# Low parts of three weights by accumulating transfers, and a new order of steps, in the first tiles of a ConvFFN

## The chip, the cores and the metric

The kernel runs on one core of one Trainium2 chip. The metric is the device time of one execution in microseconds (us); lower is better. Beside each other on the core work TensorE (matrix products; PE in the profile), VectorE (DVE), ScalarE (ACT), GpSimd (POOL) and SyncE (SP). The last issues most of the transfers between the chip's large memory and its working memory; GpSimd issues some.

## The reference

One step of a decoder layer in float32: an adaptive norm, one wide projection that feeds a short gated convolution and a windowed attention, a gated merge, a residual, and then the part that matters here, the ConvFFN, followed by a last norm:

```python
h2 = _rmsnorm(x, norm2_g) * (1.0 + sc2) + sh2
a, val = jnp.split(h2 @ w_up, 2, axis=-1)
ac, new_ffn = _causal_conv(a, ffn_buf, ffn_conv_w)
x = x + g2 * ((jax.nn.gelu(ac, approximate=False) * val) @ w_down)
```

There are 512 prompt tokens and 64 sample tokens (8 sequences of 8), 576 columns together. The model width is 1024, the inner width 2816, so `w_up` has 2 x 2816 columns: 22 gate tiles `a` and 22 value tiles `val` of 128 columns each. The causal convolution has three taps.

## The kernel before

**Products of split numbers.** TensorE multiplies numbers of a shortened float32 form (`F32R`). To keep the accuracy of float32, each operand is split into a high part (its rounding to that form) and a low part (the number minus the high part), and each product is made of three passes: high by high, high by low, low by high (`kstep`, with the weight's low part in the third pass). For a weight tile of 128 x 1024 the high part is one ScalarE pass (`whi` in the profile) and the low part one VectorE subtraction (`wlo`).

**Tiles.** Activations lie transposed: 128 features on the partitions, 576 tokens along the row. Weights arrive in tiles `raw` of 1024 x 128 (512 KB), issued by SyncE (`load_w`) into a ring of four buffers, so that a load waits until the last reader of its buffer is done. High and low parts have rings of five. A product of one weight tile with all eight feature tiles of `h2` fills one of two wide accumulators (`mm`); there are four narrow ones (`aux`).

**The stage.** The ConvFFN goes through the 22 tiles in three groups. The tiles 0 to 3 (class `FfnTile`) are plain products. All later ones (`FfnPair`) use a scheme with seven smaller products for a gate tile and a value tile together (`pair_product`, parts 1 to 7), whose operands are sums and differences of halves: of the activations (`PairOperands`, four of them, with `sums`, `high`, `low` and `n3`) and of two weight tiles (`pair_weights`, whose steps `sums1`, `sums2`, `ah`, `al`, `bh`, `bl`, `ch`, `cl`, `dh`, `dl` make the high (h) and low (l) parts of four weight sets A to D). Beside the products of the tiles 0 to 3, VectorE and ScalarE thus have to finish those tiles, prepare the four operands, and prepare the weights of pair 4.

A plain tile needs, in turn: `copies` (ScalarE takes the gate product from its accumulator into a padded row; GpSimd clears and fills the padding and keeps the convolution's state), `first_tap` (ScalarE), `taps` (two VectorE instructions), `gelu` (ScalarE), `times` (VectorE multiplies by the value product out of its accumulator), `high` (ScalarE) and `low` (VectorE). The helpers `start` and `value` are `copies` with `first_tap`, and `times` with `high`.

**What comes before.** The gate and value products of tile 0 (`acc2[0]`, `acc2[1]`) and the gate product of tile 1 (`first[2]`) are made while `h2` is still being normalised. Then follow five products over all of `h2`: `v1` (value of tile 1), `a2`, `v2`, `a3`, `v3` (gate and value of tiles 2 and 3), and after them pair 4. The weights of `v1` and `a2` are split early; those of `v2`, `a3` and `v3` in the stage itself, by `w_split`. With two wide accumulators, `v1` takes the one that tile 0's `copies` has read, `a2` the one that tile 0's `times` has read, `v2` the one of `v1`, and so on.

**What sets the order.** In this stage the lists of TensorE, VectorE and ScalarE are pinned to the order in which the program is written (`pinned`). Each engine works its list in turn, and an instruction that waits holds up all behind it. GpSimd's order is set by a scheduler at build time.

Of the kernel before, what the change touches and what calls it, by code (L numbers as in the profile page):

```python
# [10 lines left out]
F32 = mybir.dt.float32  # L11
F32R = mybir.dt.float32r
AF = mybir.ActivationFunctionType
ALU = mybir.AluOpType
AX = mybir.AxisListType

P = 128
D = 1024
NK = D // P
# [16 lines left out]
S_BUFS = 5  # L36
# [33 lines left out]
def step_kernel(ctx: ExitStack, tc: tile.TileContext, ins: dict, outs: list):  # L70
# [6 lines left out]
    wp = ctx.enter_context(tc.tile_pool(name="wp", bufs=3))  # L77
# [8 lines left out]
    def nm(s):  # L86
        cnt[0] += 1
        return f"{s}{cnt[0]}"

    def slot(s, dt=F32, shape=None):  # L90
        return ap_.tile(shape or [P, NT], dt, tag="a", name=nm(s))

    def mmps():
        return pm.tile([P, 1024], F32, tag="mm", name=nm("mm"))
# [19 lines left out]
    pe, act, dve, pool = (InOrder(e) for e in (nc.tensor, nc.scalar, nc.vector, nc.gpsimd))  # L114
# [5 lines left out]
    def pf(ps):  # L120
        return ps[:, 256:832]
# [4 lines left out]
    def sv(t):  # L126
        return t[:, 512:576]

    def b8(t):
        return t.rearrange("p (b t) -> p b t", b=8)  # L130
# [4 lines left out]
    def split(hi, lo, src):  # L135

        act.activation(hi, src, AF.Copy)
        dve.tensor_tensor(out=lo, in0=src, in1=hi.bitcast(F32), op=ALU.subtract)
# [6 lines left out]
    def load_w(src, nk):  # L145

        raw = wp.tile([P, nk, P], F32, tag="raw", name=nm("raw"), bufs=W_BUFS)
        nc.sync.dma_start(raw, src)
        return raw

    def split_w(raw):
        nk = raw.shape[1]
        hi = wp.tile([P, nk, P], F32R, tag="whi", name=nm("whi"), bufs=S_BUFS)
        lo = wp.tile([P, nk, P], F32R, tag="wlo", name=nm("wlo"), bufs=S_BUFS)
        split(hi, lo, raw)
        return (lambda k: hi[:, k, :]), (lambda k: lo[:, k, :])

    def split_w_slots(raw):

        nk = raw.shape[1]  # L160
        parts = []
        for k0 in range(0, nk, 4):
            n = min(4, nk - k0)
            hi, lo = slot("wh", F32R, [P, n, P]), slot("wl", F32R, [P, n, P])
            split(hi, lo, raw[:, k0 : k0 + n, :])
            parts.append((hi, lo))
        return (lambda k: parts[k // 4][0][:, k % 4, :]), (lambda k: parts[k // 4][1][:, k % 4, :])
# [11 lines left out]
    def tick():  # L179

        ticks[0] += 1
        if filler:
            filler[2] += filler[1]
            while filler and filler[2] >= 1.0:
                filler[2] -= 1.0
                if next(filler[0], True):
                    filler.clear()
# [6 lines left out]
    def kstep(dst, w, xs, k, groups=(0, 1)):  # L194

        hi, lo = w
        xh, xl = xs[k]
        first, last = k == 0, k == len(xs) - 1
        for wt, x, st, sp_ in ((hi(k), xh, first, False), (hi(k), xl, False, False), (lo(k), xh, False, last)):
            for g in groups:  # L200
                matmul(dst[g], wt, x[:, GRP[g][0] : GRP[g][1]], start=st, stop=sp_)

    def halves(ps):
        return ps[:, 256:512], ps[:, 512:832]

    def product(w, xs):
        ps = mmps()
        for k in range(len(xs)):
            kstep(halves(ps), w, xs, k)
            tick()  # L210
        return pf(ps)
# [17 lines left out]
    class PairOperands:  # L229
# [38 lines left out]
        def low(self):  # L268
            for lo, src, hi in ((self.tl, self.t, self.th), (self.nl, self.r[0][:, :HT], self.nh)):
                dve.tensor_tensor(out=lo, in0=src, in1=hi.bitcast(F32), op=ALU.subtract)  # L270
# [58 lines left out]
    def in_turn(t):  # L329

        order = {0: "sums1 ah al", 2: "dh dl sums2", 3: "bh bl", 4: "ch cl"}
        return {at: (lambda names=names: [t[n]() for n in names.split()]) for at, names in order.items()}
# [46 lines left out]
    def kpm(w, m0, k0=0, nk=NK):  # L379
        return w[k0 * P : (k0 + nk) * P, m0 : m0 + P].rearrange("(k p) m -> p k m", p=P)  # L380
# [7 lines left out]
    first = sp.tile([P, 1], F32, tag="first", name="first", bufs=1)  # L388
# [226 lines left out]
    def early_high(w, x):  # L615
        c, m = slice(4 * x, 4 * x + 4), slice(w * P, w * P + P)
        src = early_q[:, c, :] if w == 2 else early[x][:, :, m]
        hi, lo = wk_parts[w]
        hi, lo = hi[:, c, :], lo[:, c, :]
        act.activation(hi, src, AF.Copy)  # L620
        return lambda: dve.tensor_tensor(out=lo, in0=src, in1=hi.bitcast(F32), op=ALU.subtract)
# [29 lines left out]
    low = early_high(1, 0)  # L651
# [42 lines left out]
    for j in (2, 0, 1):  # L694
        t = slot("kT")
# [20 lines left out]
    for raw in raws:  # L716
        hi = wp.tile([P, 4, 256], F32R, tag="whi", name=nm("whi"), bufs=S_BUFS)
        lo = wp.tile([P, 4, 256], F32R, tag="wlo", name=nm("wlo"), bufs=S_BUFS)
# [14 lines left out]
    for i in range(5):  # L733
        ps = aux()
        for k in range(NK):
            whi, wlo = (x[:, k % 4, :] for x in wv[k // 4])
# [9 lines left out]
    for i in (3, 4):  # L746
# [3 lines left out]
        t = slot("kout", shape=[P, 256])  # L750
# [21 lines left out]
    def queries(t, ps=None):  # L772
# [52 lines left out]
        out=sel,  # L825
        in0=snk.rearrange("p (h g) -> p h g", h=4),
        in1=ind.unsqueeze(1).to_broadcast([P, 4, 4]),
        op=ALU.mult,
# [239 lines left out]
    def b10(t):  # L1068
        return t[:, 514:594].rearrange("p (b e) -> p b e", b=8)
# [105 lines left out]
    for m in range(NK):  # L1175
# [17 lines left out]
        if m == 1:  # L1193
# [9 lines left out]
            out=b10(u)[:, :, 2:10], in0=b8(sv(ps)), in1=b8(sv(c_sb)), op=ALU.mult  # L1203
# [52 lines left out]
    w, steps = pair_weights(*raws[0])  # L1256
    steps = in_turn(steps)
# [12 lines left out]
    def gated(m):  # L1270

        if sg[m] is not None:
            dve.tensor_tensor(out=ya[m], in0=ya[m], in1=sg[m], op=ALU.mult)
            sg[m] = None

    for n in range(len(gate_cols)):
        if n + 1 < len(gate_cols):
            gate_raws(n + 2)
            after, steps = pair_weights(*raws[n + 1])
            steps = in_turn(steps)  # L1280
# [3 lines left out]
        else:  # L1284
            w_next[0] = weights(kpm(wao, 0), NK)
            raw = load_w(kpm(wao, P), NK)
            steps = {
                0: lambda: gated(6), 1: lambda: gated(7), 3: lambda: part_o(2), 4: lambda: part_o(3),
                5: lambda: w_next.update({1: split_w(raw)}), 6: lambda: part_o(5), 7: lambda: part_o(7),
            }  # L1290
# [8 lines left out]
    for m in range(NK):  # L1299
# [5 lines left out]
        t = gb[m]  # L1305
# [62 lines left out]
    h2 = [(slot("2h", F32R), slot("2l", F32R)) for _ in range(NK)]  # L1368
# [216 lines left out]
    def down_load(m, m0, m1):  # L1585
        return load_w(kpm(w_dn, m * P, m0, m1 - m0), m1 - m0)
# [3 lines left out]
    acc2 = [mmps() for _ in range(2)]  # L1590
    first = [halves(x) for x in acc2] + [None]
# [27 lines left out]
    tiles = [FfnTile(m) for m in range(4)]  # L1619
    ops = [PairOperands(h2, kp, made2, h2_raw) for kp in range(4)]  # L1620

    def w_split(raw):
        hi, lo = (wp.tile([P, NK, P], F32R, tag=t, name=nm(t), bufs=S_BUFS) for t in ("whi", "wlo"))
        act.activation(hi, raw, AF.Copy)
        low = lambda: dve.tensor_tensor(out=lo, in0=raw, in1=hi.bitcast(F32), op=ALU.subtract)
        return ((lambda k: hi[:, k, :]), (lambda k: lo[:, k, :])), low

    def start(t, ps):
        t.copies(ps)
        t.first_tap()  # L1630

    def value(t, ps):
        t.times(ps)
        t.high()

    raw = [load_w(kpm(w_up, c), NK) for c in (FF + 2 * P, 3 * P)]
    start(tiles[0], pf(acc2[0]))
    ops[0].sums()
    tiles[0].taps()
    w_v2, low = w_split(raw[0])  # L1640
    tiles[0].gelu()
    low()
    v1 = product(w_v1, h2)
    value(tiles[0], pf(acc2[1]))
    start(tiles[1], first[2])
    tiles[0].low()
    tiles[1].taps()
    for g, k in pend[-1 - NORM2[2] :]:
        norm2_whole(g, k)
    ops[0].high()  # L1650
    tiles[1].gelu()
    w_a3, low = w_split(raw[1])
    raw = load_w(kpm(w_up, FF + 3 * P), NK)
    pair = FfnPair(4)
    ops[0].low()
    ops[1].sums()
    value(tiles[1], v1)
    low()
    ops[1].high()
    a2 = product(w_a2, h2)  # L1660
    tiles[1].low()
    ops[1].low()
    ops[2].sums()
    v2 = product(w_v2, h2)
    start(tiles[2], a2)
    ops[2].high()
    tiles[2].taps()
    w_v3, low = w_split(raw)
    tiles[2].gelu()
    low()  # L1670
    ops[2].low()
    steps = pair.prepare()
    nxt = FfnPair(5)
    ops[3].sums()
    ops[3].high()
    steps["ah"]()
    a3 = product(w_a3, h2)
    value(tiles[2], v2)
    tiles[2].low()
    ops[3].low()  # L1680
    steps["sums1"]()
    steps["al"]()
    steps["dh"]()
    steps["bh"]()
    steps["dl"]()
    v3 = product(w_v3, h2)
    start(tiles[3], a3)
    steps["sums2"]()
    tiles[3].taps()
    tiles[3].gelu()  # L1690
    steps["ch"]()
    steps["bl"]()
    steps["cl"]()
    value(tiles[3], v3)
    tiles[3].low()

# [2 lines left out]
    for m0, m1 in FCH:  # L1699
# [3 lines left out]
        for m in range(max(m0, 4), m1):  # L1703
# [6 lines left out]
            else:  # L1710
                wd = {}
                raw = [down_load(j, m0, m1) for j in range(2)]
# [11 lines left out]
        if m1 < NF:  # L1724
            pairs = {m1: FfnPair(m1)}
            steps = None
# [9 lines left out]
            for m in range(2, NK):  # L1736
# [3 lines left out]
                if m == 4:  # L1740
                    steps = in_turn(pairs[m1].prepare())
# [113 lines left out]
```

## Time and profile before

| | |
|---|---|
| median of 3 runs | 1000.4 us (1000.04 to 1001.07) |
| the profiled execution | 1001.41 us, of it span 999.6 us |
| granted TensorE clock | 0.997 |
| transferred | 119.18 MB, mean 119 GB/s |

The span is the time from the first to the last instruction of one profiled execution; the page of the profile and all queries of the trace belong to that execution. A row of a timeline gives the start, the duration, the engine, the source line, the operation, and the tile written and the tiles read (`out<-in`), with their shape; `x4` merges several like it, and square brackets give the idle time ahead of it and what ended it. Source line 109 is that of a helper through which all pinned engines are called, so tiles tell the instructions apart: `whi` and `wlo` weight parts, `y` the convolution, `cy` the multiplied tile, `fh` and `fl` its parts, `tw`, `th`, `tl` the pair operands, `pad` the padded row, `p` and `uv` the sums inside a pair.

### The profile page before, as it was taken

How to read it: one execution, taken by the hardware profiler on the slowest of the kernel's cores; microseconds unless marked ns; L12 is line 12 of the kernel's file. 1: busy time of each engine (PE TensorE's matmuls, PEld its weight loads, DVE VectorE, ACT ScalarE, POOL GpSimd, SP SyncE). 2: the span in 40 equal slices, each digit the busy share in tenths (PEclk: the TensorE clock that was granted, in tenths of full speed). 3: DMA queues.
4: the chain of work that ended last, by engine and by line, in shares of the span. 5: the costliest groups of instructions: out<-in, count | busy, mean ns of one | idle time of the engine just before them, and what ended most of it. 6: DMA issues, size and time to landing. Idle time of an engine off the chain costs nothing.

```text
span 999.6 us, 18691 instructions
## 1 busy us (share of the span) xinstructions
PE 983.2 (98%) x7516; PEld 941.8 (94%) x7516; DVE 670.7 (67%) x1241; ACT 450.8 (45%) x835; POOL 100.3 (10%) x271
## 2 busy tenths in 40 slices
PE   7999999999999999999999999999999999999997
PEld 5899999999999989999889999999999999999997
DVE  5736676676463348788454568896569995579953
ACT  5454555545334225545232347554225552235453
POOL 2221101020000000000000021011001110001120
PEclk9999999999999999999999999999999999999999
DMA  9984332233421752235972302223233222323302
GB/s 290 319 253 109 86 90 70 86 116 115 141 76 53 246 180 85 86 106 157 338 231 72 106 11 75 65 85 106 85 101 90 85 85 86 106 65 101 110 10 95
DMA packets 173481, 119.18 MB, mean 119 GB/s; under 512 B 6887, under 2 KB 160846, under 8 KB 173106
## 3 DMA queue, kind: packets, MB, share of 16 engines
q1 hardware_dynamic: 169954, 107.00, 35.3%
q0 software_dynamic: 3296, 10.73, 3.5%
q8 instruction: 59, 0.97, 0.4%
q14 instruction: 28, 0.23, 0.1%
q10 hardware_dynamic: 144, 0.26, 0.1%
HBM read 109.17 MB, written 7.35 MB: 117 GB/s over the span
## 4 chain that ended last, share of the span: by engine, by line
PE 82%; DVE 10%; issue 2%; DMA 2%; ACT 2%; SPq 0%; POOL 0%; POOLq 0%; DVEq 0%; ACTq 0%
PE mm L109 60%; PE aux L109 19%; DVE wlo L109 3%; PE aux L1116 2%; DMA ad<-in_w_ada 2%; PE aux L1016 2%; DVE raw L109 1%; DVE uv L109 1%; DVE y L109 1%; DVE cy L109 1%; DMA raw<-in_w_in 1%; DVE fl L109 1%; SPq L385 0%; DVE wl L109 0%; ACT whi L109 0%
## 5 line engine op out<-in xcount | busy, mean ns | idle before, releaser
L109 ACT ACTIVATE whi<-raw 128x1024 fp32r<-128x1024 f32 (+2 forms) x164 | 168.1, 1034 | 178.6 <-PE mm L109 95.5
L109 DVE TENSOR_TENSOR wlo<-raw,whi 128x1024 fp32r<-128x1024 f32 (+2 forms) x164 | 195.1, 1194 | 48.6 <-ACT whi L109 47.9
L109 PE MATMUL mm<-hh,whi 128*128 128x256 f32 (+2 forms) x560 | 124.6, 299 | 0.6 <-ACT hh L109 0.6
L109 PE MATMUL mm<-hh,wlo 128*128 128x256 f32 (+2 forms) x560 | 121.8, 294 | 0.0
L109 PE MATMUL mm<-hl,whi 128*128 128x256 f32 (+2 forms) x560 | 121.0, 295 | 0.1
L109 PEld LDWEIGHTS mm<-hh,whi 128*128 128x128 f32 x560 | 93.0, 188 | 2.9 <-ACT hh L109 1.2
L109 PEld LDWEIGHTS mm<-hh,wlo 128*128 128x128 f32 x560 | 94.2, 188 | 0.0
L109 PEld LDWEIGHTS mm<-hl,whi 128*128 128x128 f32 x560 | 93.6, 188 | 0.5 <-DVE hl L109 0.5
L109 DVE SCALAR_TENSOR_TENSOR x<-mm,modT,x 128x512 f32<-128x512 f32 (+1 forms) x33 | 22.6, 686 | 71.1 <-PE mm L109 71.0
L109 PE MATMUL mm<-fh,whi 128*128 128x256 f32 (+1 forms) x304 | 65.0, 296 | 0.3 <-DVE rt L109 0.3
L109 PE MATMUL mm<-fl,whi 128*128 128x256 f32 (+1 forms) x304 | 65.1, 295 | 0.0
L109 PE MATMUL mm<-fh,wlo 128*128 128x256 f32 (+1 forms) x304 | 64.9, 295 | 0.0
L109 PE MATMUL mm<-th,whi 128*128 128x288 f32 x208 | 61.7, 297 | 0.7 <-DVE uv L109 0.7
L109 PE MATMUL mm<-th,wlo 128*128 128x288 f32 x208 | 61.6, 296 | 0.6 <-DVE wlo L109 0.6
L109 PE MATMUL mm<-tl,whi 128*128 128x288 f32 x208 | 61.4, 295 | 0.0
L109 PEld LDWEIGHTS mm<-fh,whi 128*128 128x128 f32 x304 | 50.7, 188 | 0.5 <-PE mm L109 0.5
L109 PEld LDWEIGHTS mm<-fl,whi 128*128 128x128 f32 x304 | 51.0, 188 | 0.0
L109 PEld LDWEIGHTS mm<-fh,wlo 128*128 128x128 f32 x304 | 50.8, 188 | 0.0
L867 ACT ACTIVATE s<-s,nmx 128x256 f32<-128x256 f32 (+1 forms) x72 | 34.0, 474 | 32.0 <-DVE nmx L864 31.2
L109 PE MATMUL aux<-2h,whi 128*128 128x288 f32 (+2 forms) x160 | 47.2, 295 | 0.8 <-ACT p L109 0.8
L109 PE MATMUL aux<-2h,wlo 128*128 128x288 f32 (+2 forms) x160 | 47.3, 296 | 0.0
L109 PE MATMUL aux<-2l,whi 128*128 128x288 f32 (+2 forms) x160 | 47.0, 294 | 0.0
(310 smaller groups left out, 2568.8 us busy)
## 6 DMA issues: line engine op xcount, KB each, us to landing
raw<-in_w_in SPq DMA_DIRECT2D x52, 512.0 KB, 4.2
raw<-in_w_up SPq DMA_DIRECT2D x44, 512.0 KB, 3.9
ada<-in_w_ada SPq DMA_DIRECT2D x64, 256.0 KB, 6.0
ad<-in_w_ada SPq DMA_DIRECT2D x32, 256.0 KB, 6.3
raw<-in_w_down SPq DMA_DIRECT2D x16, 512.0 KB, 3.5
raw<-in_w_conv_out SPq DMA_DIRECT2D x8, 512.0 KB, 3.5
raw<-in_w_attn_out SPq DMA_DIRECT2D x8, 512.0 KB, 4.2
raw<-in_w_mix_out SPq DMA_DIRECT2D x8, 512.0 KB, 6.1
```

Source lines behind the costliest of these rows:

```text
L109: done = getattr(self.engine, name)(*args, **kwargs)
L867: nc.scalar.activation(s[x // 2][:, x % 2, :w], s[x // 2][:, x % 2, :w], AF.Exp, bias=nmx[:, x : x + 1], accum_out=den[:, x : x + 1],)
L1016: done = nc.tensor.matmul(O[HALF[par], :256], vt(i - nkt + 1 + kt)[:, hd * 64 : hd * 64 + 64], pts[kt][:, par * 256 : par * 256 + 256], st ...
L1116: done = nc.tensor.matmul(ps[32 * j : 32 * j + 32, :], cT[:, k, :], cols[k][j], start=(k == 1), stop=(k == NK - 2),)
```

## The change

The low part of three weights, those of `v2`, `a3` and `v3`, is made another way. ScalarE writes minus the high part into the tile `lo`: a pass over `raw` with scale -1, rounded to the same form. Then GpSimd issues a transfer from `raw` to `lo` that adds what it carries to what lies there. Sum and difference are the same number as before. The third pass of a product now waits for the transfer, and so does the load that takes the buffer of `raw`.

The order of the steps is rewritten from the start of the stage to the pair products. Tile 0 and tile 1 go through their steps side by side; the pair operands and the steps of pair 4's weights are placed anew between the tiles' steps. The order of the products, and with it TensorE's list, remains, as does SyncE's list of loads. GpSimd's list has the padding of tile 1 earlier, and the three transfers: two between the state copies of tile 1 and the padding of tile 2, one between the state copies of tile 2 and the padding of tile 3.

```diff
+    def w_split_adding(raw):
+
+
+        hi, lo = (wp.tile([P, NK, P], F32R, tag=t, name=nm(t), bufs=S_BUFS) for t in ("whi", "wlo"))
+        act.activation(hi, raw, AF.Copy)
+
+        def low():
+            act.activation(lo, raw, AF.Copy, scale=-1.0)
+            pool.dma_start(lo, raw, accum_op=ALU.add)
+
+        return ((lambda k: hi[:, k, :]), (lambda k: lo[:, k, :])), low
...
-    def w_split(raw):
-        hi, lo = (wp.tile([P, NK, P], F32R, tag=t, name=nm(t), bufs=S_BUFS) for t in ("whi", "wlo"))
-        act.activation(hi, raw, AF.Copy)
-        low = lambda: dve.tensor_tensor(out=lo, in0=raw, in1=hi.bitcast(F32), op=ALU.subtract)
-        return ((lambda k: hi[:, k, :]), (lambda k: lo[:, k, :])), low
...
     raw = [load_w(kpm(w_up, c), NK) for c in (FF + 2 * P, 3 * P)]
-    start(tiles[0], pf(acc2[0]))
+    tiles[0].copies(pf(acc2[0]))
+    tiles[1].copies(first[2])
     ops[0].sums()
-    tiles[0].taps()
-    w_v2, low = w_split(raw[0])
-    tiles[0].gelu()
+    for t in tiles[:2]:
+        t.first_tap()
+    for t in tiles[:2]:
+        t.taps()
+    w_v2, low = w_split_adding(raw[0])
+    for t in tiles[:2]:
+        t.gelu()
     low()
     v1 = product(w_v1, h2)
     value(tiles[0], pf(acc2[1]))
-    start(tiles[1], first[2])
-    tiles[0].low()
-    tiles[1].taps()
+    value(tiles[1], v1)
+    ops[1].sums()
+    for t in tiles[:2]:
+        t.low()
+    ops[0].high()
     for g, k in pend[-1 - NORM2[2] :]:
         norm2_whole(g, k)
-    ops[0].high()
-    tiles[1].gelu()
-    w_a3, low = w_split(raw[1])
+    w_a3, low = w_split_adding(raw[1])
+    low()
     raw = load_w(kpm(w_up, FF + 3 * P), NK)
     pair = FfnPair(4)
     ops[0].low()
-    ops[1].sums()
-    value(tiles[1], v1)
-    low()
     ops[1].high()
+    ops[2].sums()
     a2 = product(w_a2, h2)
-    tiles[1].low()
     ops[1].low()
-    ops[2].sums()
-    v2 = product(w_v2, h2)
     start(tiles[2], a2)
     ops[2].high()
     tiles[2].taps()
-    w_v3, low = w_split(raw)
     tiles[2].gelu()
+    w_v3, low = w_split_adding(raw)
     low()
-    ops[2].low()
+    ops[3].sums()
     steps = pair.prepare()
     nxt = FfnPair(5)
-    ops[3].sums()
+    ops[2].low()
+    steps["ah"]()
     ops[3].high()
-    steps["ah"]()
-    a3 = product(w_a3, h2)
+    v2 = product(w_v2, h2)
+    steps["sums1"]()
+    steps["dh"]()
     value(tiles[2], v2)
+    steps["al"]()
+    ops[3].low()
     tiles[2].low()
-    ops[3].low()
-    steps["sums1"]()
-    steps["al"]()
-    steps["dh"]()
     steps["bh"]()
     steps["dl"]()
+    steps["sums2"]()
+    steps["bl"]()
+    a3 = product(w_a3, h2)
+    start(tiles[3], a3)
+    steps["ch"]()
+    tiles[3].taps()
+    steps["cl"]()
+    tiles[3].gelu()
     v3 = product(w_v3, h2)
-    start(tiles[3], a3)
-    steps["sums2"]()
-    tiles[3].taps()
-    tiles[3].gelu()
-    steps["ch"]()
-    steps["bl"]()
-    steps["cl"]()
     value(tiles[3], v3)
     tiles[3].low()
```

## The prediction

> **What bounds the kernel now.** I read the page's first part, then the busy times by stage, then TensorE's waits with its timeline, and last the chain of waits through the one stretch where TensorE waits.
>
> ```profile
> span 999.6 us, 18691 instructions
> PE 983.2 (98%) x7516; PEld 941.8 (94%) x7516; DVE 670.7 (67%) x1241; ACT 450.8 (45%) x835; POOL 100.3 (10%) x271
> ...
> 606.00:637.00 31.00, 31.00 (x235) 31.00 (x234) 26.28 (x47) 21.46 (x38) 2.47 (x13) 1.00 0.20 58
> 637.00:647.00 10.00, 8.54 (x63) 8.07 (x62) 8.58 (x14) 5.52 (x10) 1.92 (x6) 1.00 0.36 104
> ```
>
> TensorE is busy for 98% of the span, so only its idle time can be won. The columns of the two stage rows are length, then busy time of TensorE, its weight loads, VectorE, ScalarE and GpSimd. The steps that the change touches run beside 606 to 647. Up to 637 TensorE has no gap. Its 1.46 us of idle time lie between 637 and 647.
>
> ```profile
> 641.68 0.29 PE L109 MATMUL mm<-th,whi 128*128 128x288 f32 x1
> ...
> 642.72 0.40 PE L109 MATMUL mm<-th,wlo 128*128 128x288 f32 x1 [0.62 <-DVE wlo L109]
> ...
> 646.74 0.40 PE L109 MATMUL aux<-2h,whi 128*128 128x288 f32 x1 [0.84 <-ACT p L109]
> ...
> 654.94 3.17 PE mm L109 x24
> ...
> 666.04 3.17 PE mm L109 x24
> ...
> 677.32 3.41 PE mm L109 x24
> ```
>
> These are the second parts of the pair products 4, 5, 6 and 7. The first stall (0.62) waits for the low part of pair 4's third weight tile, `cl`; the second (0.84) for ScalarE's copy of the first part's bank. Start to start it is 654.94 - 641.68 = 13.26 us, then 11.10, then 11.28. An undisturbed pair takes 11.10, so pair 4 loses **2.16 us** (the two gaps and the slower restart after each) and pair 6 to 7 loses 0.18. Nothing else in the touched stage costs TensorE time: the most that this change can win is 2.34 us.
>
> ```profile
> 641.44 1.22 DVE wlo L109
> 642.67 0.74 DVE cy L109 x2
> 643.43 0.69 ACT fh L109
> 644.12 1.34 ACT 2h L109 x4
> 645.46 0.95 ACT whi L109
> 646.40 0.29 ACT p L109
> ```
>
> The chain of waits says why: VectorE's list is late. `cl` ends at 642.66, behind it come tile 3's multiplication (cy), its high part (fh), four `n3` passes (2h), the next pair's `ah` and only then the bank's copy.
>
> **The change, part by part.** TensorE's list and SyncE's stay as they are. VectorE loses three passes, ScalarE gains three, GpSimd gains three transfers; the rest is order.
>
> ```profile
> L109 ACT ACTIVATE whi<-raw x20: 1042/1047/1063, 608.2 to 697.6; 128x1024 fp32r<-128x1024 f32 x20
> L109 DVE TENSOR_TENSOR wlo<-raw,whi x18: 1212/1218/1226, 610.0 to 692.7; 128x1024 fp32r<-128x1024 f32 x18
> ...
> 606.81 0.70 ACT L109 COPY pad<-mm 128x512 f32<-128x512 f32 x2 [0.92 <-PE mm L109]
> 607.55 0.79 ACT L109 ACTIVATE y<-pad,par2T 128x592 f32<-128x592 f32 x1
> 608.24 1.05 ACT L109 ACTIVATE whi<-raw 128x1024 fp32r<-128x1024 f32 x1
> 609.31 1.28 ACT L109 ACT_TABLE_LOAD   x1
> 610.60 0.70 ACT L109 ACTIVATE y<-y 128x592 f32<-128x592 f32 x1
> ...
> 614.31 1.69 ACT L109 ACTIVATE t<-t,modT 128x256 f32<-128x256 f32 x4
> ...
> 614.44 1.71 DVE L109 SCALAR_TENSOR_TENSOR y<-pad,par2T,y 128x592 f32<-128x592 f32 x2 [0.77 <-ACT y L109]
> ...
> 619.25 0.81 DVE L109 TENSOR_TENSOR cy<-mm,y 128x512 f32<-128x512 f32 x2
> 619.99 1.21 DVE L109 TENSOR_TENSOR wlo<-raw,whi 128x1024 fp32r<-128x1024 f32 x1
> 621.12 0.75 DVE L109 TENSOR_TENSOR fl<-cy,fh 128x576 fp32r<-128x576 f32 x1
> ...
> 608.37 0.42 PE L109 MATMUL mm<-2h,wh 128*128 128x256 f32 x2
> ...
> 621.61 0.43 PE L109 MATMUL mm<-2h,wlo 128*128 128x256 f32 x2
> ...
> 640.09 0.30 PE L109 MATMUL aux<-2h,whi 128*128 128x288 f32 x1
> ```
>
> *VectorE:* 3 x 1.13 us (619.99 to 621.12, start to start) = 3.4 us less before pair 4. *ScalarE:* 3 minus passes of 1.05 us = 3.15 us more, on 21.46 busy of 31: it has the room, if none delays what others wait for.
>
> I play the new lists with these durations (successive passes of one engine start some 0.1 us before the earlier ends). TensorE's five products v1, a2, v2, a3, v3 take (640.09 - 608.37) / 5 = 6.34 us each; they start at 608.37, 614.71, 621.06, 627.40, 633.75, and pair 4 at 640.09.
>
> ScalarE: both tiles' copies end at 609.0 (tile 1's second bank is full only near 608.5), two first taps to 610.4, `w_v2`'s high part to 611.4, table load to 612.65, gelu 0 to 613.3, gelu 1 (tile 1's taps on VectorE end at 613.1) to 613.9, **minus pass to 614.9**. VectorE multiplies tile 0 from 613.4 to 614.2; a2 needs that bank at 614.71: 0.5 us to spare, so the later tile 0 costs nothing. Tile 1's multiplication follows v1 and ends at 615.8, 5 us before v2 wants the bank. Then ScalarE: fh twice and th, nh to 617.4, four norm passes to 619.0, `w_a3` high to 620.0 and **minus to 620.9**; th, nh of pair operand 1, tile 2's copies to 622.4, its tap to 623.2. GpSimd's list has the second transfer ahead of tile 2's padding, so the padding waits until 621.5, still ahead of the tap; behind the third stands tile 3's padding, wanted at 634 only. Tile 2's taps keep VectorE to 624.9, gelu to 625.7, `w_v3` high to 626.6 and **minus to 627.6**.
>
> The three transfers are issued at 614.93, 620.93 and 627.63. TensorE reads the first low part in each product's third pair of passes, 0.54 us after its start (621.61 against 621.07): at 621.60, 627.94, 634.29. So a transfer has 6.67, 7.01 and 6.66 us.
>
> **What a transfer takes** no row shows, since none accumulates.
>
> ```profile
> 141.93 0.53 POOL L769 DMA_DIRECT2D kh<-kh  x1 [10.94 <-ACT kh L109]
> DMA to landing us min/median/max: 2.2/2.2/2.2
> 142.90:143.60 0.70, 0.70 (x8) 0.70 (x7) 0.09 (x2) 0.70 (x5) 0.14 (x1) 1.00 0.83 187
> ...
> DMA to landing us min/median/max: 7.4/7.4/7.4
> ...
> x<-xT_dram POOLq DMA_DIRECT2D x2, 1152.0 KB, 9.0
> raw<-in_w_up SPq DMA_DIRECT2D x2, 512.0 KB, 3.8
> ```
>
> Nearest is GpSimd's 128 KB copy within the chip's memory: 2.2 us alone (row 141.93), its data moving at 187 GB/s for 0.7 us, so 1.5 us around the data; with the queues full the same kind took 7.4. From below: 2.2. From above: 9.0, 1152 KB with all queues busy. Mine lies between: 512 KB at 187 GB/s are 2.8 us, and reading the target as well makes up to twice that, 5.6, so 7.1 in all; but a weight load of 512 KB, four times this copy's bytes over twice its partitions, lands in 3.8. I take **5.0 us**, 1.5 plus 3.5, between these two. The second and third meet one weight load each (3.8 us alone, freed by the transfer before). That leaves 1.7, 2.0 and 1.7 us, and the stall is nothing.
>
> The three deadlines do not add up. Each minus pass follows ScalarE's and VectorE's work, not the product that waits: if the first transfer is late by d, everything on TensorE moves by d, and the second and third gain d of room. So the price is once (landing time - 6.67): nothing at 2.2 or 5.0, 2.3 us at 9.0.
>
> **Afterwards.** VectorE: tile 2's multiplication at 628.8, `al` to 630.7, `sums2` at 633.0, tile 3's taps 635.5 to 637.2, **`cl` to 638.3** where pair 4 wants it at 641.9. The first stall goes. v3 ends near 640.3; multiplication to 641.1, fh to 641.8, `n3` to 643.1, `ah` to 644.1, **bank copied by 644.4**; part 4 would start at 640.09 + 3 x 1.586 = 644.85. The second stall goes, by 0.4 us. On SyncE's queue three loads now wait for the transfers where they waited for VectorE's low parts, since each takes the buffer that a transfer reads: pair 4's second weight (619.9 + 3.8 = 623.7, wanted by `sums1` at 627.5) and pair 5's two (629.7 and 636.4, wanted near 643). None is late. VectorE comes some 2.4 us earlier to the next pair's steps and TensorE 2.16, so the 0.18 between pairs 6 and 7 stays or goes; I count it as staying.
>
> **Sum.** The profiled execution took 1001.41 us, 1.8 beyond its span and 1.0 above the median of 1000.4. From it: 1001.41 - 2.16 = 999.25. From the median, against which the result stands: 1000.4 - 2.16 = **998.2 us**.
>
> **The rivals.**
> *Late transfers.* GpSimd issues these transfers while VectorE runs nearly without a pause, and VectorE slows GpSimd.
>
> ```profile
> 637.38 0.19 POOL L1094 COPY sto<-pad 128x16 f32<-128x16 f32 x1
> ...
> 638.15 0.77 POOL L1491 COPY pad<-stF 128x16 f32<-128x16 f32 x1
> ```
>
> Two like copies, 0.19 and 0.77 us, the long one under VectorE's taps. If a transfer waits so for two VectorE instructions of 1.22 us, it lands after 5.0 + 2.4 = 7.4, 0.8 late: 999.0; with 8.8 the gain is gone. Against it: the 2.2 us copy was issued beside the same kind of VectorE work. The Trainium skill, "SBUF — State Buffer", section "Who interferes with whom", puts this as a lock: GpSimd shares a port pair with VectorE, and while VectorE holds it in a two-port mode no descriptor is written; it blames copies and scalar forms, and spares two-tensor forms because those take only the read side. By that rule these transfers would not wait, as the VectorE rows here are TENSOR_TENSOR and SCALAR_TENSOR_TENSOR; by its 3.1 us against 0.62 for the blocked case, an estimate of 7.5 us would come out, and 999.0. No run here shows an accumulating one.
>
> *Slower: the accumulation itself is slow.* If the engines add at a quarter of 187 GB/s, the data takes 11.2 us and a transfer lands after 12.7: v2 waits 6.0 us, and as the transfers come only 6.0 and 6.7 us apart, each queues behind the last and the next two deadlines slip by nearly 5 more each. 1000.4 - 2.16 + 6.0 = 1004.3 if they overlap freely, near 1014 if they queue. It decides from a landing of 8.8 us on (slower than before) and passes 0.2% at 10.8. For it: nothing in this trace adds in flight. Against: each engine would have to move its share four times slower than in row 141.93.
>
> *The stalls stay.* Part 4 has only 0.4 us. If ScalarE, with 3.15 us more, is 0.8 late with `n3` or `ah`, the 0.84 stays or VectorE's delay shows up at the pair's bank six instead: 998.2 + 1.1 = 999.3.
>
> **How the numbers follow.** Forecast 0.62, late transfers 0.12, slow accumulation 0.16, stalls that stay 0.10. About 0.2% (2 us) is what a measurement of this kernel can tell from no change; faster by it means under 998.4. The forecast's own range is 997.6 to 998.9, which I put 0.45 under and 0.17 above that line. Faster 0.45; same 0.17 + 0.12 + 0.10 = 0.39; slower 0.16. Range: from 997.5 to 1001.4, a landing near 9.8 us and so beyond the upper row; the slow accumulation is left out.
>
> **What would show it.** Right: the three transfers land under 6.6 us, no gap before the low parts' matmuls in v2, a3 and v3, `cl` done by 639, no gap in pair 4, second parts 11.1 us apart from pair 4 on. Wrong: TensorE waiting for a transfer into wlo; transfers of 8 us or more; a gap at a2's start (tile 0 too late) or at the fourth part of pair 4.

## The result and the profile after

The changed kernel takes 998.59 us (median of 12 runs, 997.72 to 999.19) where the kernel before, measured beside it, takes 1000.61 (12 runs, 1000.04 to 1001.46): 2.02 us less, a ratio of 0.9979 with a 95% interval of 0.997 to 0.9988, so a gain of 1.2 to 3.0 us. The 0.2% by which the prediction told faster from no change lie inside this interval, and the median stands on that line (998.6); that there is a gain at all is clear. The profiled execution took 998.56 us. Its page begins:

```profile
span 996.8 us, 18698 instructions
...
PE 982.1 (99%) x7516; PEld 941.9 (94%) x7516; DVE 666.7 (67%) x1238; ACT 453.1 (45%) x838; POOL 102.8 (10%) x274
```

VectorE has three instructions fewer and 4.0 us less to do, ScalarE three more and 2.3 us more. TensorE works through the same 7516 matmuls. Of the 2.8 us between the two spans, 1.7 were its idle time and 1.1 its busy time (983.2 against 982.1). The first matmul behind a gap lasts longer, 0.40 us against 0.29 in the prediction's rows, so a gap costs more than its idle time. The windows of the touched stage (length, then TensorE, its weight loads, VectorE, ScalarE, GpSimd) show where:

```profile
606.00:637.00 31.00, 31.00 (x236) 31.00 (x235) 25.97 (x46) 25.38 (x43) 6.38 (x19) 1.00 0.45 107
637.00:647.00 10.00, 10.00 (x78) 10.00 (x77) 7.29 (x14) 5.67 (x11) 0.00 (x0) 1.00 0.31 94
```

The 1.46 us of idle time between 637 and 647 are gone. The chain that ended last is now TensorE alone from 600 to 690. The first matmul of the second part of the pairs 4 to 7 starts, in the timeline after:

```profile
641.07 0.29 PE L109 MATMUL mm<-th,whi 128*128 128x288 f32 x1
...
652.19 0.30 PE L109 MATMUL mm<-th,whi 128*128 128x288 f32 x1
...
663.32 0.29 PE L109 MATMUL mm<-th,whi 128*128 128x288 f32 x1
...
674.49 0.37 PE L109 MATMUL mm<-th,whi 128*128 128x288 f32 x1
```

The same matmuls before (pair 4's, at 641.68, stands in the prediction):

```profile
654.78 0.29 PE L109 MATMUL mm<-th,whi 128*128 128x288 f32 x1
...
665.88 0.29 PE L109 MATMUL mm<-th,whi 128*128 128x288 f32 x1
...
677.32 0.37 PE L109 MATMUL mm<-th,whi 128*128 128x288 f32 x1 [0.17 <-DVE uv L109]
```

They are now 11.12, 11.13 and 11.17 us apart, where they were 13.10, 11.10 and 11.44. Pair 4 gained 1.98 us and the step from pair 6 to 7 gained 0.27. (The 13.26 of the prediction takes its first end from the timeline and its second from the chain of waits, whose piece begins 0.16 later than its first matmul.) The timeline shows the new steps: the three transfers, the matmuls that want them, and then `cl`, tile 3's multiplication, the bank's copy and part 4 of pair 4.

```profile
614.62 0.94 POOL L109 DMA_DIRECT2D wlo<-raw  x1 [5.91 <-ACT wlo L109]
620.62 0.88 POOL L109 DMA_DIRECT2D wlo<-raw  x1 [5.06 <-ACT wlo L109]
627.35 0.86 POOL L109 DMA_DIRECT2D wlo<-raw  x1 [5.10 <-ACT wlo L109]
...
621.00 0.43 PE L109 MATMUL mm<-2h,wlo 128*128 128x256 f32 x2
...
627.34 0.43 PE L109 MATMUL mm<-2h,wlo 128*128 128x256 f32 x2
...
633.68 0.43 PE L109 MATMUL mm<-2h,wlo 128*128 128x256 f32 x2
...
636.61 1.22 DVE L109 TENSOR_TENSOR wlo<-raw,whi 128x1024 fp32r<-128x1024 f32 x1
639.75 0.82 DVE L109 TENSOR_TENSOR cy<-mm,y 128x512 f32<-128x512 f32 x2 [1.93 <-PE mm L109]
...
643.49 0.38 ACT L109 COPY p<-aux 128x288 f32<-128x288 f32 x1
...
644.24 0.29 PE L109 MATMUL aux<-2h,whi 128*128 128x288 f32 x1
```

This trace stands 0.61 us ahead of the one before: the first low part in v2 is read at 621.00, there at 621.61. That much of the 2.8 us between the spans arose ahead of the touched stage and is no part of the gain. From issue to the matmul that wants it a transfer has 6.38, 6.72 and 6.33 us. The view of these instructions alone says how long they took:

```profile
DMA to landing us min/median/max: 4.5/4.7/5.1
```

So each is there 1.2 us or more ahead. `cl` ends at 637.83 and the bank's copy at 643.87, 0.37 us before part 4 starts. VectorE, which was behind before, now waits 1.93 us for v3.

### The profile page after: what moved, and what is told of

Its sections match the earlier page's. It is cut to its first block, busy times and chain, and to the rows that moved or that the text cites. A ratio compares the mean times of both kernels' runs of the same rounds, so it can differ in the third digit from the quotient of the medians.

```text
span 996.8 us, 18698 instructions
## 1 busy us (share of the span) xinstructions
PE 982.1 (99%) x7516; PEld 941.9 (94%) x7516; DVE 666.7 (67%) x1238; ACT 453.1 (45%) x838; POOL 102.8 (10%) x274
## 4 chain that ended last, share of the span: by engine, by line
PE 93%; DVE 2%; DMA 2%; issue 1%; ACT 1%; POOL 0%; POOLq 0%; DVEq 0%; SPq 0%; ACTq 0%
PE mm L109 68%; PE aux L109 22%; PE aux L1128 2%; PE aux L1028 2%; DMA raw<-in_w_in 1%; DVE wlo L109 1%; DMA ad<-in_w_ada 1%; DMA x<-in_x_prompt 0%; DVE ol L109 0%; DVE uv L109 0%; ACT oh L109 0%; DVE raw L109 0%; DVE fl L109 0%; DVE cy L109 0%; DVE sg L109 0%
## 5 line engine op out<-in xcount | busy, mean ns | idle before, releaser
L109 DVE TENSOR_TENSOR wlo<-raw,whi 128x1024 fp32r<-128x1024 f32 (+2 forms) x161 | 191.5, 1194 | 47.6 <-ACT whi L109 47.1
```

The source lines that it names most:

```text
L109: done = getattr(self.engine, name)(*args, **kwargs)
```

## The experiments

Every run is compared with runs of the kernel before on the same chip. Its median there was 1000.7, 1000.65 and 1000.55 us in the three groups: e1 to e4, e5 to e8, e9 to e11.

### e1 and e2: each part alone

The order of the changed kernel with VectorE's subtraction in the place of minus pass and transfer (e1), and the other way round (e2):

```diff
 # e1, the changed kernel with
-            act.activation(lo, raw, AF.Copy, scale=-1.0)
-            pool.dma_start(lo, raw, accum_op=ALU.add)
+            dve.tensor_tensor(out=lo, in0=raw, in1=hi.bitcast(F32), op=ALU.subtract)
```

```diff
 # e2, the kernel before with
-        low = lambda: dve.tensor_tensor(out=lo, in0=raw, in1=hi.bitcast(F32), op=ALU.subtract)
+        def low():
+            act.activation(lo, raw, AF.Copy, scale=-1.0)
+            pool.dma_start(lo, raw, accum_op=ALU.add)
```

> The new order of steps, but the three low parts by VectorE's subtraction as in the kernel before. Theory (the gain needs both the 3.4 us taken from VectorE and the order): played with the durations of the rows, the three passes put VectorE's last weight step for pair 4 back to about 642, so a stall of 0.3 to 0.6 us ahead of pair 4's second part stays, the fourth part waits again some 0.8 us, and tile 0's multiplication comes about 0.2 us late for a2: 0.2 to 0.9 us under the kernel before, near 1000.0. Rival (the order alone does it, the transfers are idle ornament): 2.0 us under it, 998.6, no wait of TensorE in pair 4. Rival (the order costs and only the transfers pay): over 1000.6.

> The old order of steps, but the three low parts by minus pass and accumulating transfer. Theory: VectorE is free of 3.4 us, but in the old order ScalarE's high part of the third weight set stands behind tile 3's gelu, so the low part still ends near 642: 0.7 to 1.3 us under the kernel before, near 999.6, and the wait of the fourth part of pair 4 stays at 0.6 to 0.9 us. Rival (the transfers alone do it): 2.0 us under it, 998.6. Rival (ScalarE's three more passes cost): over 1000.6.

Neither gains: e1 took 1000.79 us (ratio 1.0002, 0.9993 to 1.001), e2 1000.55 (0.9996, 0.9987 to 1.0005). I had expected 1000.0 and 999.6, and missed by 0.8 and 0.9. The timeline of e1 with TensorE's waits, two of the subtractions and `cl`:

```profile
614.61 0.51 PE L109 MATMUL mm<-2h,wh 128*128 128x256 f32 x2 [0.25 <-DVE cy L109]
...
619.50 1.23 DVE L109 TENSOR_TENSOR wlo<-raw,whi 128x1024 fp32r<-128x1024 f32 x1 [1.28 <-ACT whi L109]
...
627.74 1.22 DVE L109 TENSOR_TENSOR wlo<-raw,whi 128x1024 fp32r<-128x1024 f32 x1 [1.72 <-ACT whi L109]
...
641.15 1.22 DVE L109 TENSOR_TENSOR wlo<-raw,whi 128x1024 fp32r<-128x1024 f32 x1
...
642.42 0.40 PE L109 MATMUL mm<-th,wlo 128*128 128x288 f32 x1 [0.17 <-DVE wlo L109]
646.44 0.40 PE L109 MATMUL aux<-2h,whi 128*128 128x288 f32 x1 [0.84 <-ACT p L109]
```

Both stalls are there, the first smaller than before, the second at its full 0.84, and ahead of them is a wait of 0.25 for tile 0's multiplication, which stands behind the first subtraction. The next two rows are new as well: here the subtraction comes right behind the high part in the lists, so VectorE stands for 1.28 and 1.72 us until ScalarE has made it, and everything behind on VectorE's list stands with it. In e2 the chain of waits shows another holder:

```profile
638.92 0.70 ACT y L109
639.63 0.95 ACT whi L109
...
640.60 1.23 DVE wlo L109
```

VectorE has three passes less, but in the old order the high part of pair 4's third set (`ch`) stands behind gelu 3 on ScalarE's list. `cl` gets its input at 640.58, and TensorE waits 0.23 and 0.85.

### e3 and e4: the transfers later

The calls of `low()` moved behind later steps: the first alone (e3), all three (e4).

```diff
 # e3
-    low()
     v1 = product(w_v1, h2)
 ...
         norm2_whole(g, k)
+    low()
     w_a3, low = w_split_adding(raw[1])
```

```diff
 # e4: the first as in e3, and
     w_a3, low = w_split_adding(raw[1])
-    low()
 ...
     ops[2].high()
+    low()
     tiles[2].taps()
     tiles[2].gelu()
     w_v3, low = w_split_adding(raw)
-    low()
 ...
     steps["bh"]()
+    low()
     steps["dl"]()
```

> As the changed kernel, but the minus pass for v2's low part comes after tile 0's and 1's high parts, the first operand's and the four norm passes, so the first transfer is issued near 618.5 instead of 614.6. Theory (a late transfer costs what it is late, once): it lands near 623.2 to 623.6 where TensorE wants it at 621.0, so 2.2 to 2.6 us over the changed kernel, near 1001.0; the second and third transfer are not waited for. Rival (transfers have more room than thought, or the product is not held up): under 0.5 us over the changed kernel.

> As the run with the first transfer late, and the minus passes of the other two set later as well: each would by itself land about 1.5 us (a3) and 2.1 us (v3) after TensorE wants it in the changed kernel. Theory (deadlines do not add, since the first delay gives the others room): the same as the run with the first alone late within 0.5 us, near 1001.0. Rival (each late transfer costs its own): 2.3 + 1.5 + 2.1 = 5.9 us over the changed kernel, near 1004.5.

e3 took 1003.67 us (1.0022, 1.0013 to 1.0031; the runs lie between 1001.52 and 1004.29), e4 1005.12 (1.0046, 1.0033 to 1.006). Both lie far above the expectation of 1001.0. In e3's timeline the transfer and the matmul that waits for it:

```profile
620.30 0.94 POOL L109 DMA_DIRECT2D wlo<-raw  x1 [10.97 <-ACT wlo L109]
624.86 0.54 PE L109 MATMUL mm<-2h,wlo 128*128 128x256 f32 x2 [3.07 <-DMA wlo<-raw]
```

In e4's the matmuls that wait, and what stands ahead of the third transfer:

```profile
623.95 0.53 PE L109 MATMUL mm<-2h,wlo 128*128 128x256 f32 x2 [3.06 <-DMA wlo<-raw]
...
631.65 0.82 DVE L109 TENSOR_TENSOR cy<-mm,y 128x512 f32<-128x512 f32 x2 [2.69 <-PE mm L109]
...
632.51 0.69 ACT L109 ACTIVATE fh<-cy 128x576 fp32r<-128x576 f32 x1 [3.60 <-DVE cy L109]
...
634.05 1.04 ACT L109 ACTIVATE wlo<-raw 128x1024 fp32r<-128x1024 f32 x1
...
635.38 0.87 POOL L109 DMA_DIRECT2D wlo<-raw  x1 [9.60 <-ACT wlo L109]
...
639.86 0.53 PE L109 MATMUL mm<-2h,wlo 128*128 128x256 f32 x2 [1.45 <-DMA wlo<-raw]
```

The transfers were set later than I had meant, and e4 doesn't test what it was built for. In the prediction no minus pass hangs on a product that waits. Here the third one stands behind tile 2's high part (fh), which needs tile 2's multiplication (cy), which needs all of v2, the product that the first transfer had held up: VectorE stood 2.69 us for it. Against an undisturbed course (a low part is read 0.27 us after the pair of matmuls ahead of it began, here at 620.46, and v3's two products of 6.34 after v2's) the first low part comes 3.2 us late and the third 6.45. Without the 2.69 the third would have been some 3.8 late, an estimate. So what is paid here is neither the 3.2 nor the 3.8 but nearly both together: a late input that itself waits for the product held up adds to the first. e3, with one wait, cost 5.1 us by the medians and only 4.0 in the profiled execution, for a transfer 3.2 late; the last section comes back to this.

### e5: what adding costs

```diff
-            pool.dma_start(lo, raw, accum_op=ALU.add)
+            pool.dma_start(lo, raw)
```

> The three transfers of the changed kernel carry raw to the low tile without adding, so the three low parts become copies of the weights. Question: what adding costs. Theory: reading the target beside the source takes time, as the prediction put it; a plain copy of 512 KB lands in 3.3 to 4.0 us against the 4.5, 4.7 and 5.1 us of the adding ones. Rival: a transfer of this size takes as long either way, 4.4 us or more. The kernel's time stays at 998.6 by both, since none of the three is waited for.

The view of the transfers in e5:

```profile
DMA to landing us min/median/max: 2.8/2.9/3.0
```

A plain copy of 512 KB lands in 2.9 us, the adding one in 4.7: adding costs 1.8 us. Its issue also holds GpSimd longer, 0.86 to 0.94 us against 0.53 to 0.62. The Trainium skill, "DMA: Bandwidth & Descriptors", section "Anatomy of one DMA — SWDGE (gpsimd) path", fits a transfer issued by GpSimd with 2.0 us plus the bytes at 436 GB/s, 3.2 us for this size; the plain copies agree within 0.4. The one run of e5 took 998.74 us.

### e7: all three a little late

A copy of half of `raw` onto itself goes ahead of each adding transfer, which waits for it.

```diff
+            pool.dma_start(raw[:, :4, :], raw[:, :4, :])
             pool.dma_start(lo, raw, accum_op=ALU.add)
```

> The changed kernel with a copy of half of raw onto itself (256 KB) ahead of each adding transfer, on the same queue; the adding one waits for it. Each chain takes some 2.9 + 4.7 us from the first issue, 7.6 with the second issue some 7.9, and has 6.4, so that each of the three is 1.2 to 1.5 us late by itself. Theory (deadlines do not add): TensorE waits once, before v2's low part, and the kernel takes 998.6 + 1.4 = 1000.0 (999.5 to 1000.7). Rival (each costs): 998.6 + 3 x 1.4 = 1002.8 (1002 to 1003.5). A wait this short should leave the granted clock at 1.00.

It took 999.99 us (0.9995, 0.9986 to 1.0004), 1.4 more than the changed kernel, as the theory had it; three prices would have been 1002.8. TensorE's waits in the timeline:

```profile
621.54 0.54 PE L109 MATMUL mm<-2h,wlo 128*128 128x256 f32 x2 [0.84 <-DMA wlo<-raw]
...
635.06 0.53 PE L109 MATMUL mm<-2h,wlo 128*128 128x256 f32 x2 [0.58 <-DMA wlo<-raw]
```

I had expected one wait, and there are two. The three minus passes run as in the changed kernel (on this trace's clock 0.45 to 0.47 us earlier, all three), so here no transfer depends on the product that waits. Undisturbed, reckoned as for e4 from the pair of matmuls that began at 620.27, the low parts would be read at 620.54, 626.88 and 633.22; they are there at 621.54, 627.77 (issued at 622.67, 5.1 us to landing) and 635.06, so 1.0, 0.9 and 1.8 us late, 3.7 together. The first wait moves TensorE and gives the other two as much room: the second is not waited for at all, and the third costs only the rest. At the third matmul TensorE is 1.8 us behind, the greatest lateness of the three. The 1.4 of the medians fits it within the interval.

### e8: the end of the new order, with the transfers

e2 with the steps after `bh` and `dl` as in the changed kernel:

```diff
-    v3 = product(w_v3, h2)
-    start(tiles[3], a3)
     steps["sums2"]()
+    steps["bl"]()
+    start(tiles[3], a3)
+    steps["ch"]()
     tiles[3].taps()
+    steps["cl"]()
     tiles[3].gelu()
-    steps["ch"]()
-    steps["bl"]()
-    steps["cl"]()
+    v3 = product(w_v3, h2)
```

> The order of before with the three minus passes and adding transfers, and of the new order only the end: sums2, bl, tile 3's copies, ch, taps, cl, gelu. Theory: with the transfers alone cl was held by ScalarE, which made ch behind gelu 3; with this one move cl ends by 640 and the bank's copy by 644.5, both stalls go, and the rest of the new order was not needed: 998.6 (998.2 to 999.3). Rival: the earlier steps (tiles 0 and 1 side by side, the operands placed anew) carry the gain as well, and 1000.0 to 1000.6 remains.

It took 999.4 us (0.9991, 0.9982 to 0.9999), between the two expectations. The first stall is gone; of the second the timeline keeps

```profile
644.11 0.41 PE L109 MATMUL aux<-2h,whi 128*128 128x288 f32 x1 [0.66 <-ACT p L109]
```

So, with the transfers in place, `ch` ahead of gelu 3 and `cl` ahead of the wait for v3 carry some 1.2 of the 2 us (1000.65 - 999.4), and the earlier steps in their new places the rest.

### e6 and e9: one subtraction in two places

The changed kernel with the low part of the third weight by VectorE again (`w_split_vector` is `w_split` of before). In e6 the subtraction stands where the minus pass stood, in e9 two VectorE steps later:

```diff
 # e6 and e9
-    w_v3, low = w_split_adding(raw)
+    w_v3, low = w_split_vector(raw)
-    low()                       # the minus pass and transfer
+    low()                       # e6: here
     ops[3].sums()
     steps = pair.prepare()
     nxt = FfnPair(5)
     ops[2].low()
+    low()                       # e9: here
```

> The changed kernel with the low part of the third weight (v3) made by VectorE's subtraction again, in the place of its minus pass. VectorE gets 1.13 us back ahead of pair 4. Theory (the 0.4 to 0.5 us before part 4 of pair 4 is not VectorE's to lose): VectorE waits 1.93 us for v3 between cl and tile 3's multiplication, so cl ends near 639.0 instead of 637.8 and all behind it stays: 998.6 (998.1 to 999.1). Rival: the delay goes through to the copy of the first part's bank, 0.5 us are there, 0.6 are missing, and after the restart some 0.6 to 1.1 us are lost: 999.2 to 999.7.

> As e6 (third low part by VectorE's subtraction), but placed two VectorE steps later, behind pair operand 2's low parts, when ScalarE's high part is long done. Theory: e6 lost because the subtraction waited 1.71 us for ScalarE's high part and held VectorE's list; without that wait VectorE is only 1.13 us later, cl ends near 639.0 on the clock of the changed kernel's trace, before v3's end at 639.75, and nothing is lost: 998.6 (998.2 to 999.0). Rival: VectorE's 1.13 us count by themselves, 999.2 as in e6.

e6 took 999.19 us (0.9985, 0.9976 to 0.9994): the rival's figure. I had left a wait out. Its timeline:

```profile
626.91 1.22 DVE L109 TENSOR_TENSOR wlo<-raw,whi 128x1024 fp32r<-128x1024 f32 x1 [1.71 <-ACT whi L109]
...
645.60 0.41 PE L109 MATMUL aux<-2h,whi 128*128 128x288 f32 x1 [0.42 <-ACT p L109]
```

The subtraction costs VectorE 1.71 us of waiting and 1.13 of work, more than the 1.93 that VectorE has before tile 3's multiplication. In e9 the same subtraction finds its high part ready. e9 took 998.49 us (0.9979, 0.9969 to 0.9988), with no gap in TensorE from 606 to 680: the work by itself costs nothing, the place did. The intervals of e6 and e9 overlap, so it is the traces that show this: pair 4 takes 11.81 us in e6 and 11.12 in e9.

### e10 and e11: the transfers taken back

Two (e10, the second weight keeps its transfer) and all three low parts (e11) by VectorE's subtraction, each in a place where the high part is done:

```diff
 # e11; e10 is the same without the two lines for w_a3
+    w_v2, low = w_split_vector(raw[0])
 ...
     ops[1].sums()
+    low()
 ...
+    w_a3, low = w_split_vector(raw[1])
 ...
     ops[2].sums()
+    low()
 ...
+    w_v3, low = w_split_vector(raw)
 ...
     ops[2].low()
+    low()
```

> As e9, and the first weight's low part too by VectorE's subtraction, behind pair operand 1's sums, where its high part is done; only the second weight keeps the adding transfer. Of its 1.13 us VectorE's wait of 0.64 before tile 2's taps takes up part, so that cl comes 1.6 us later than in the changed kernel, near 639.5, still before 639.75. Theory (VectorE has 1.93 us before tile 3's multiplication): 998.7 (998.2 to 999.2). Rival (the relief of VectorE by all three is needed): 999.5 to 1000.3.

> As e10, and the second weight's low part too by VectorE's subtraction, behind pair operand 2's sums: the new order with no minus pass and no transfer, as in e1, but with each subtraction where its high part is done. VectorE comes to tile 3's multiplication some 2.5 to 2.9 us later than cl ended in the changed kernel (637.8), 0.6 to 1.0 after v3's end, against 0.5 us to spare. Theory: cl is in time, the first stall stays away, the second comes back with 0.1 to 0.5 us: 999.2 (998.7 to 999.7). Rival (it is the transfers that are needed): both stalls, 1000.3 to 1000.8 as in e1.

e10 took 998.2 us (0.9975, 0.9966 to 0.9985) and e11 998.51 (0.9979, 0.997 to 0.9988). e11 has no minus pass and no transfer, the same passes as the kernel before, and a gain that the times can't tell from that of the changed kernel. Its timeline: the three subtractions, `cl`, the bank's copy, the matmuls that want these two, and the first matmuls of the second parts of pair 4 (640.90) and pair 5 (652.25):

```profile
616.53 1.22 DVE L109 TENSOR_TENSOR wlo<-raw,whi 128x1024 fp32r<-128x1024 f32 x1
...
621.72 1.22 DVE L109 TENSOR_TENSOR wlo<-raw,whi 128x1024 fp32r<-128x1024 f32 x1
...
628.14 1.22 DVE L109 TENSOR_TENSOR wlo<-raw,whi 128x1024 fp32r<-128x1024 f32 x1
...
638.91 1.22 DVE L109 TENSOR_TENSOR wlo<-raw,whi 128x1024 fp32r<-128x1024 f32 x1
...
640.90 0.29 PE L109 MATMUL mm<-th,whi 128*128 128x288 f32 x1
...
641.16 0.29 PE L109 MATMUL mm<-th,wlo 128*128 128x288 f32 x1
...
643.77 0.38 ACT L109 COPY p<-aux 128x288 f32<-128x288 f32 x1
...
644.20 0.40 PE L109 MATMUL aux<-2h,whi 128*128 128x288 f32 x1
...
652.25 0.30 PE L109 MATMUL mm<-th,whi 128*128 128x288 f32 x1
```

No subtraction has a wait ahead of it. `cl` is done at 640.13, 1.0 us early; the bank's copy ends at 644.15, only 0.05 before part 4 starts, and part 4 starts 0.13 late: 3.30 us behind the first matmul of the second part, against 3.17 in the changed kernel. Pair 4 takes 11.35 us instead of 11.12. So the second stall is back with 0.2 us, as the theory had it, while the time came out better than its range. The traces order the runs by the length of pair 4, first matmul of its second part to that of pair 5, and the medians go along, each known to within a microsecond:

| | pair 4, us | median against the kernel before, us |
|---|---|---|
| the kernel before | 13.10 | |
| e2, transfers only | 12.71 | -0.15 |
| e1, order only | 12.68 | +0.09 (with the wait ahead of a2) |
| e8, end of the order, transfers | 12.03 | -1.25 |
| e6, third subtraction too early | 11.81 | -1.46 |
| e11, three subtractions placed | 11.35 | -2.04 |
| e9, third subtraction placed | 11.12 | -2.06 |
| e10, first and third placed | 11.11 | -2.35 |
| the changed kernel | 11.12 | -2.02 |

e9 to e11 and the changed kernel can't be told apart by their times, so none is offered as better.

## Why the prediction was right, point by point

- *What bounds the kernel, and the most that can be won.* Right in what stalls and in the whole, wrong by 0.16 in how it is split. The 13.26 us for pair 4 mixes two views; by the timeline alone it is 13.10, so pair 4 lost 2.00 and not 2.16, and the step from pair 6 to 7 lost 0.34 and not 0.18. The 2.34 in all stand, and the sum should have read 1000.4 - 2.00 = 998.4. Of these, pair 4 gave back 1.98 and the other step 0.27; the 2.02 measured, known to about a microsecond, agrees with either.
- *VectorE and ScalarE.* Played with the durations of before, the new lists came out within 0.15 us: on this trace's clock the forecast for `cl` is 637.7 (measured 637.83) and for the bank's copy 643.8 (643.87). ScalarE's minus passes delayed nothing, as counted. Part 4 had 0.4 us to spare in the forecast and 0.37 in the trace.
- *When the transfers are issued.* Forecast 614.3, 620.3 and 627.0 on this clock, measured 614.62, 620.62 and 627.35: each 0.3 late, out of a reserve of over 1 us. The minus passes end when forecast (614.31, 620.32, 627.04); the time from ScalarE's end to GpSimd's issue is what the sum left out.
- *What a transfer takes.* 5.0 us was chosen between 3.8 and 7.1, and 4.5 to 5.1 was measured. That the adding takes time of its own holds: e5 puts it at 1.8 us of 4.7. But 187 GB/s was too slow a rate for such a copy: by it the plain one would take 1.5 + 2.8 = 4.3 us, and it took 2.9. The choice of a middle value made up for that, so the size was partly luck. Any landing under 6.3 us would have met all three.
- *Three deadlines do not add.* In the changed kernel none of the three is waited for, so the result itself doesn't test this. e7 does: 1.8 paid at the third matmul, the greatest of 1.0, 0.9 and 1.8. The text said that a price comes once, for the first transfer; more exactly, it is the greatest lateness of the three. e4 shows the condition, which the text did state: no minus pass may hang on the product that waits.
- *The loads behind the transfers and the pairs after.* No wait for a load appears in the stage. The loss between the pairs 6 and 7, which the sum left standing, went for the most part, 0.27 of 0.34 us.
- *The rivals.* Late transfers: the longest landed 1.2 us early or more, so VectorE beside them did not hold them up by the 2.4 us of that rival. By the rule cited there ("SBUF — State Buffer" of the Trainium skill: forms with two tensors leave GpSimd's descriptors alone) that was to be expected, and the trace agrees with its 4.5 to 5.1 us. Slow accumulation needed 8.8. Of the stalls that stay nothing was seen.
- *What the prediction left out.* It priced VectorE's relief as 3 x 1.13 us and read the two parts of the change as one thing. The sum was right, but the three passes are not what had to go. e11 keeps them all in the new order and loses 0.2 us in pair 4, which its time doesn't show, since VectorE has room for them; e1 keeps them in the place of the minus passes and loses everything, since there the second and third also make VectorE wait for ScalarE. The second cost, 1.28 + 1.72 = 3.0 us in e1, is nearly as large as the passes' own 3.4, and without it these fit. A minus pass has no such wait, because ScalarE makes both parts itself; that is what the transfers are worth here, besides some 0.3 us more of reserve before part 4 (0.37 against 0.05) and the 0.2 us in pair 4. And by e2 the transfers are worth nothing without the new order.

## What to carry to other kernels

In a list that an engine works in turn, an instruction costs its duration and the wait for its input, and the second depends on its place alone: look for a place where the input is long done before you move the work to another engine. Several late inputs of one busy engine cost the greatest lateness among them, not the sum, as long as the later inputs don't depend on the engine's own progress; where one does, as in e4, it adds. Before crediting the part of a change that looks clever, put the plain version into the new order.

## What the hardware showed besides

After the wait of 3.06 us in e4, the windows of the trace show TensorE's granted clock (the column before the last two) at half for some 3 us:

```profile
622.00:624.00 2.00, 0.05 (x1) 0.06 (x1) 1.52 (x2) 2.00 (x4) 0.00 (x0) 1.00 0.67 131
624.00:626.00 2.00, 2.00 (x11) 2.00 (x12) 1.97 (x6) 2.00 (x4) 1.22 (x3) 0.67 0.38 104
626.00:628.00 2.00, 2.00 (x10) 2.00 (x9) 1.24 (x3) 1.68 (x3) 0.00 (x0) 0.50 1.18 289
628.00:630.00 2.00, 2.00 (x17) 2.00 (x16) 0.93 (x2) 0.63 (x1) 0.00 (x0) 0.98 0.67 131
```

TensorE runs 10 matmuls in 2 us there instead of 17. This was paid for: v2 ends later by it, and with v2 the multiplication and the third transfer behind it. Idle times of 3.06 and 1.45 us leave some 1.9 of the 6.45 for slower matmuls, most of it in these windows. The profiled execution of e3 had a wait of 3.07 us and kept its clock at 1.00; it took 1002.54 us, where e3's median is 1003.67. The Trainium skill, "TensorE: Matmul & The Clock Gate", Part 1, puts a gate on the clock that halves it after an idle window of some 3.4 us which runs freely, so that it varies with where the wait falls; a drop after 3.06 us in one execution and none after 3.07 in another fits the second half of this, while the idle time seen is shorter than the window. That most runs of e3 lost some of their time this way is argued from their spread, not shown, since one execution of each was profiled. A lateness of 3 us can thus cost more than 3, as e4's windows show; the 0.84 and 0.58 of e7 left the clock alone.
